# Layer 1 of a two-layer attention backbone: key copies, input splits and weight loads issued at other places

## The chip, the core and the metric

One core of a Trainium2 chip runs the whole kernel in one launch. The time is the device time of the launch in microseconds (us). TensorE (PE in the profile) does matmuls and transposes, VectorE (DVE), ScalarE (ACT) and GpSimd (POOL) do elementwise work, and SyncE (SP) issues most DMAs; ACT issues a few. Each engine executes its own list of instructions in the order in which the program was written out, and waits at an instruction whose inputs aren't there. The output is compared with a reference in fp32.

## The reference

1024 latent tokens of width 1024 (a 16 x 64 grid) and 256 context tokens go through two layers, each `x = x + gate * mixer(rms_norm(x))` with a modulation from a conditioning vector.

- Layer 0 projects to two attentions with grouped heads (one global, one in a window of 128) with rotary embedding, a SiLU gate on each, and an output projection.
- Layer 1 projects to a convolution branch (512 channels, 31 taps, layer norm, SiLU gates) and to a neighbourhood attention "d" (8 heads of 64, each query of the grid sees 8 rows x 16 columns and the context, with a bias table). Both branches are concatenated and projected:

```python
oc = conformer_conv(cv, cgl, cg, dw_w, dw_b, ln_g, ln_b)
...
y_lat = jnp.concatenate([oc, od * jax.nn.silu(dg)], axis=-1) @ w_out
```

- At the end stands a final RMS norm of the latent tokens. The change touches layer 1 only.

## The kernel before

**Arithmetic.** Everything is fp32. A matmul operand is split into a high and a low part (`split`: ACT writes the high part by a cast, L312, and POOL or DVE subtracts for the low part, L315), and a product is three matmuls (`mm3`, L334 to L336: high x high and the two mixed ones). Weights come in pieces of 128 x 256: `load_w` (L340) issues a DMA on SP into a raw buffer `wr` and splits it into `wh` and `wl`. There are `WPR` = 3 raw buffers, so a load waits until the split three pieces back is done.

**The order.** The kernel's text is traced once, and a scheduler that goes by dependences and modelled times then writes out each engine's list. `tc.issue_after(ins)` binds what is issued in its block on the engine of `ins` behind `ins`; otherwise the scheduler may put an instruction ahead of those that were written before it. `weave(main, n, fill, m)` steps two generators against each other: the attention (`main`), and projections that fill TensorE meanwhile (`fill`). `WV` holds the number of steps of each weave, `LAG` how far the fill is bound behind the attention's score matmuls.

**Layer 1's stages.** `d_proj(i)`, i = 0 to 3, projects q, k, v and the gate of the head pair i over three chunks of tokens (c = 1, 2 latent, 512 tokens each; c = 0 context, 256) and writes them to DRAM (QD, KD, VD, GD). The convolution is in the same part of the program, and its output goes to DRAM as Oc. Around `d_proj(1)` stands the layer norm of the convolution branch (its `uc`, `s`, `trs`). Then the attention runs through 16 groups (8 heads x 2 halves of the grid's columns, the order in `SEQ`), woven with `d_proj(2)`, `d_proj(3)`, then with the output projection of the convolution part (`out1_part(range(4))`, its matmuls are `po`), then of the first three head pairs (`out1_part((4, 5, 6), (1,))`), then with the ends.

**A group** (`attn_gen`, `group1`) has seven tiles of keys. Per tile: scores `st` on PE (L491 with the high parts KAt, L495 with the low parts in KBt), the bias added on DVE (`pf`, L500; not for the two context tiles), the exponential on ACT (L501, L503), `split` into `ph` (ACT) and `pl` (POOL, each fifth on DVE), and three matmuls `ov` on PE (L433 to L435). Ahead of a group its maxima are found (`mx` on PE, reduced with a bias `bm` on DVE into `mp`, then `nmt` and `QL`). In mid-group (tile 3) `gate()` loads the gate; at the last tile `last()` is called.

**Keys.** A head's keys are loaded by `load_head` into KAt at the start of the head before. `copy_k` (L580) copies the 64 high rows into KBt, one ACT cast of 64 x 1536 (L581). It is called for the next head in `last()` of each head's first half; the first head's by the `EARLY` table during `d_proj(1)`.

**The branches read back.** `out1_alloc` (L1446) allocates the tiles `oc`, `x2` and `od3`, and reads Oc back in eight DMAs of 128 x 512 on ACT's queue, each followed by its split (high on ACT, low on DVE). `od_load(hf)` (L1466) reads three pieces of 128 x 512 of the attention's output from O1d on SP's queue, each followed by its split (low on POOL). Both are called between weaves.

Of the kernel before, what the change touches and what calls it, by code (L numbers as in the profile page):

```python
# [10 lines left out]
F32 = mybir.dt.float32  # L11
# [7 lines left out]
P = 128  # L19
# [24 lines left out]
STG = {"pair": 2, "vT": 1, "spo": 2}  # L44
OCE, ODE, OHE = ('v', 'g', 'g')
YB = 1
WPR = 3
VS0 = 12
N0 = 9
NLAST = (48, 28)  # L50
# [15 lines left out]
SQP = ((2, 3, 4, 5, 6), (), (4, 6))  # L66
ENDS = ((0, 0, 512), (1, 0, 256), (1, 256, 256))
LATE = 100
EARLY = {2: lambda g, h, c: next(g[0].prep), 4: lambda g, h, c: h(0), 8: lambda g, h, c: c(),
         10: lambda g, h, c: next(g[1].prep), 14: lambda g, h, c: g[0].load_bs(), 18: lambda g, h, c: g[1].load_bs()}  # L70
NFILL = (34, 34, 34)
# [18 lines left out]
def tile_kernel(ctx: ExitStack, tc: tile.TileContext, a, out):  # L90
# [9 lines left out]
    solo = [True]  # L100
    turn = [0, 0]
    mk, mwp, hold, layer = [0], [None], [0], [0]
    sts, pvs = [], []

    def bank(tag, name):
        if tag == "pp" and solo[0]:
# [6 lines left out]
    def nm(s):  # L113
        uid[0] += 1
        return f"{s}_{uid[0]}"
# [300 lines left out]
    def attn_gen(pool, groups, vshare, look, nexts=None):  # L416
# [58 lines left out]
        for x, (g, t) in enumerate(items):  # L475
            if x + AHEAD < len(items):
                items[x + AHEAD][0].ahead(items[x + AHEAD][1])
            if t == 0:
                g.start()
                while any(p is g.prep for _, p in work):  # L480
                    prepare(len(items), 1)
                for k in g.ids:
                    next(preps[k])
                    work.append((x + LEAD[layer[0]], preps[k]))
            rate = g.rate * max(len(work), 1)
            k, q0, n, extra = g.tiles[t]
            KA, KB = g.k()
            st = bank("st", nm("st"))
            cs = slice(k * P, (k + 1) * P)
            sf = flat(st, q0, n)  # L490
            sts.append(PE.matmul(sf, KA[:, cs], cut(g.QH, q0, n), start=True, stop=False))  # L491
            if not g.bias:
                for lhs, rhs in extra():
                    PE.matmul(st[:, :n], lhs, rhs, start=False, stop=False)
            PE.matmul(sf, KB[0:68, cs], cut(g.QL[0:68], q0, n), start=False, stop=True)  # L495
            ph = pool.tile([P, 512], F32R, tag="ph", name=nm("ph"), bufs=look + 1)
            pl = pool.tile([P, 512], F32R, tag="pl", name=nm("pl"), bufs=look + 1)
            pf = pool.tile([P, 512], F32, tag="pf" if layer[0] else "ost", name=nm("pf"), bufs=PFB)
            if g.bias and extra is not None:
                VE.tensor_tensor(flat(pf, q0, n), sf, extra(), op=ALU.add)  # L500
                SC.activation(pf[:, :n], pf[:, :n], AF.Exp)  # L501
            else:
                SC.activation(pf[:, :n], st[:, :n], AF.Exp, scale=1.0 if g.bias else SCALE)  # L503
            cnt[0] += 1
            split(pf[:, :n], ph[:, :n], pl[:, :n], "s", "v" if cnt[0] % vshare == 0 else "g")
            pend.append((g, t, ph, pl))
            if t == len(g.tiles) // 2:
                g.gate()
            if t == len(g.tiles) - 1:
                g.last()  # L510
            prepare(x, rate // 2)
            yield
            if len(pend) > look:
                flush()
            prepare(x, rate - rate // 2)
            yield
# [63 lines left out]
    def copy_k(KA, KB):  # L580
        SC.copy(KB[0:64, :], KA[0:64, :].bitcast(F32))  # L581
# [370 lines left out]
    def pair(name, n=512, tag="pair"):  # L952
        return (stg[0] if tag == "spo" else lp).tile([P, 2, NR * NW], F32R, tag=tag, name=nm(name), bufs=STG[tag])[:, :, :n]
# [189 lines left out]
    with ExitStack():  # L1143
# [74 lines left out]
            w = ap.rearrange("p (r c) -> p r c", c=64)[:, :, NCOL[h_] : NCOL[h_] + NW]  # L1218
            return w.rearrange("p r (t j) -> p r t j", j=8)

        def d_proj(i):
            wsrc = (wp, WB)
            wh, wl = load_w(wsrc[0], a["od_d"], i * 512, 256, 256, wsrc[1])
            for c in (1, 2):
# [29 lines left out]
            for c in VORD:  # L1254
# [18 lines left out]
                for k0 in range(0, len(blocks), 4):  # L1273
                    bl = blocks[k0 : k0 + 4]
                    tr = bank(TRV, nm("trv"))
                    for k, (_, v) in enumerate(bl):
                        PE.transpose(tr[:, k * P : (k + 1) * P], v, ident)
                    sp = pair("spv", 640)
                    n = len(bl) * P
                    sv = sp.rearrange("p a b -> p (a b)").rearrange("p (j s d) -> p j s d", s=2, d=64)  # L1280
                    src = tr[:, :n].rearrange("p (j d) -> p j d", d=64)
                    split(src, sv[:, : 2 * len(bl), 1], sv[:, : 2 * len(bl), 0], "s", "v")
                    sv = sp.rearrange("p a b -> p (a b)").rearrange("p (j e d) -> p j e d", e=2, d=P)
                    k = 0
                    while k < len(bl):
                        e = k + 1
                        while e < len(bl) and bl[e][0] == bl[e - 1][0] + 1:
                            e += 1
                        SY.dma_start(VD[i][:, bl[k][0] : bl[k][0] + e - k], sv[:, k:e].bitcast(F32))
                        k = e  # L1290
                if c:
                    SY.dma_start(GD[i][:, :, (c - 1) * 256 : c * 256], sg.rearrange("p (h q) -> p h q", h=2))

# [37 lines left out]
        def group1(gi, hd, hf):  # L1331
# [24 lines left out]
            def gate():  # L1356
                g.gt = half("gt1")
                SY.dma_start(g.gt[ds], GD[i][ds, hf])

            def start():  # L1360
                for g2 in groups1[gi + 1 : gi + 2] if gi else ():
# [4 lines left out]
                    SY.dma_start(Vs[gi % 2][:, j : j + n, 0:128].bitcast(F32), VD[i][:, k : k + n, e])  # L1366

            def last():
                if hf == 0 and hd < 7:
                    copy_k(*heads[hd + 1])  # L1370

            def maxes(QH, mp):
                KA = Ks[hd % len(Ks)][0]
# [71 lines left out]

        def out1_alloc():  # L1446
            for c in range(2):
                ocs.append(bigp.tile([P, 2, 4, 512], F32R, tag="big", name=nm("oc")))
            for c in range(2):
                x2.append(bigp.tile([P, DK, 512], F32, tag="big", name=nm("x2")))  # L1450
                od3.append(pair("od3"))
            for c in range(2):
                for f in range(4):
                    lo = ocs[c][:, 1, f, :]
                    SC.dma_start(lo.bitcast(F32), Oc[:, f, c * 512 : (c + 1) * 512])
                    split(lo.bitcast(F32), ocs[c][:, 0, f, :], lo, "s", OCE)
                yield

        x2_of = {}

# [5 lines left out]
        def od_load(hf):  # L1466
            od[hf] = bigp.tile([P, 2, 3, 512], F32R, tag="big", name=nm("od"))
            for f in range(3):
                lo = od[hf][:, 1, f, :]
                SY.dma_start(lo.bitcast(F32), O1d[:, f, hf, :])  # L1470
                split(lo.bitcast(F32), od[hf][:, 0, f, :], lo, "s", ODE)

        def out1(fs, e, k, wh, wl, o=0, n=512):

# [87 lines left out]

        main = attn_gen(dpool, groups1, VSH, LOOK1, {11: [], 12: [13, 14], 13: [15]})
        weave(main, WV[0], d_proj(2), 31, False, True, LAG[0])
        weave(main, WV[1], d_proj(3), 31, False, True, LAG[1])
        run(out1_alloc())
        weave(main, WV[2], out1_part(range(4)), 32, False, True, LAG[2])
        assert fin[0] >= 12
        for hf in (1, 0):
            od_load(hf)  # L1570
        weave(main, WV[3], out1_part((4, 5, 6), (1,)), 8, False, True, LAG[3])
        assert fin[0] >= 14
        weave(main, WV[4], ends(EV0), NEV, False, True)
        wend = [load_w(wp, a["od_wo"], e2 * 256, 256, 256, WB, lambda dk: "gv"[dk % 2], dks=[7]) for e2 in range(4)]
# [123 lines left out]
```

## Time and profile before

| | us |
|---|---|
| median of three runs (lowest, highest) | 1540.65 (1538.62, 1540.72) |
| the profiled execution, its span | 1541.49, 1539.7 |
| PE busy (granted clock over the span) | 1444.9 (0.966) |
| DVE, POOL, ACT busy | 1109.2, 822.7, 757.4 |
| d_proj(1) with the layer norm | about 1115 to 1200 |
| d_proj(2), d_proj(3) with attention | about 1200 to 1345 |
| output projections with attention | about 1345 to 1500 |
| ends | 1500 to 1540 |

The places of the stages are read from the times of their first and last instructions. In the views, L12 is line 12 of the kernel, `out<-in` are the program's names, x8 a count, and `[4.34 <-DMA KAt<-KD]` the idle time ahead of an instruction and what ended it. PE's matmuls overlap in the pipeline: one of 512 columns is shown with 0.40 us, while the next begins 0.24 us after it. The clock that was granted to PE stands in the windows as a share of full speed.

### The profile page before, as it was taken

Reading aid. Unit: us, or ns where it says so; the run is one execution under the profiler, and the core shown is the slowest. Engines: PE = TensorE matmul, PEld = TensorE weight load, DVE = VectorE, ACT = ScalarE, POOL = GpSimd, SP = SyncE. Lnnn points to the kernel's source line nnn. Section 1 sums busy time; section 2 is a strip of 40 time slices with the busy share of each in tenths; the row PEclk is TensorE's granted clock in tenths of the full one; section 3 lists DMA queues with packets and bytes.
Section 4 is the critical chain, followed back from the end, with each engine's and each line's share of the span. In section 5 each row is a group of like instructions: output and inputs, shape, how many; then the busy total and the mean of one; then the engine's idle time right before and its main releaser. Section 6 shows DMA issues by size and latency. Waiting matters only on the chain.

```text
span 1539.7 us, 22012 instructions
## 1 busy us (share of the span) xinstructions
PE 1444.9 (94%) x6984; PEld 1172.4 (76%) x6984; DVE 1109.2 (72%) x2173; ACT 757.4 (49%) x1545; POOL 822.7 (53%) x762
## 2 busy tenths in 40 slices
PE   7889989999999999899999989999999999999994
PEld 2879868977788678678888767888878878877784
DVE  5899888588868667645478676999837665766766
ACT  3721353445453755565545665443434454544572
POOL 3361463555554775676555775664543443354664
PEclk9999989999999999999999999999999999999996
DMA  9567144423441123642111131213495677777623
GB/s 351 197 188 255 56 148 153 144 63 113 148 139 52 44 82 121 197 147 62 39 48 46 59 106 52 86 57 109 141 289 175 216 202 220 234 236 217 186 65 109
DMA packets 181163, 213.66 MB, mean 139 GB/s; under 512 B 17068, under 2 KB 134520, under 8 KB 181048
## 3 DMA queue, kind: packets, MB, share of 16 engines
q1 hardware_dynamic: 174384, 200.69, 41.7%
q10 hardware_dynamic: 6664, 11.57, 2.4%
q8 instruction: 55, 0.90, 0.3%
q14 instruction: 60, 0.49, 0.1%
HBM read 152.17 MB, written 60.03 MB: 138 GB/s over the span
## 4 chain that ended last, share of the span: by engine, by line
PE 71%; DVE 11%; DMA 6%; issue 5%; POOL 3%; ACT 2%; SPq 0%; ACTq 0%; DVEq 0%; POOLq 0%
PE p L336 7%; PE p L335 7%; PE p L334 7%; PE ov L433 4%; PE ov L435 4%; PE ov L434 4%; PE po L335 4%; PE po L334 4%; PE po L336 4%; PE st L495 3%; PE st L491 3%; PE pq L334 2%; PE pg L335 2%; PE pg L334 2%; PE pg L336 2%
## 5 line engine op out<-in xcount | busy, mean ns | idle before, releaser
L315 POOL TENSOR_TENSOR pl<-pf,ph 128x512 fp32r<-128x512 f32 (+3 forms) x321 | 392.6, 1234 | 284.2 <-ACT ph L312 218.7
L315 POOL TENSOR_TENSOR wl<-wr,wh 128x256 fp32r<-128x256 f32 (+2 forms) x256 | 193.0, 770 | 144.2 <-ACT wh L312 93.3
L503 ACT ACTIVATE pf<-st 128x512 f32<-128x512 f32 x284 | 167.1, 596 | 180.9 <-PE st L495 122.2
L312 ACT CAST ph<-pf 128x512 fp32r<-128x512 f32 (+3 forms) x364 | 206.8, 578 | 31.6 <-PE ov L434 22.5
L334 PE MATMUL p<-hh,wh 128*128 128x512 f32 x448 | 177.8, 400 | 1.6 <-ACT wh L312 1.4
L335 PE MATMUL p<-hl,wh 128*128 128x512 f32 x448 | 178.7, 401 | 0.4 <-POOL hl L315 0.4
L336 PE MATMUL p<-hh,wl 128*128 128x512 f32 x448 | 176.4, 402 | 2.1 <-POOL wl L315 2.0
L312 ACT CAST wh<-wr 128x256 fp32r<-128x256 f32 (+2 forms) x264 | 103.5, 404 | 134.1 <-DMA wr<-in_od_d_dram 29.9
L433 PE MATMUL ov<-ph,Vt 128*128 128x512 f32 (+3 forms) x364 | 143.3, 394 | 9.4 <-ACT ph L312 4.4
L491 PE MATMUL st<-QH,KAt 128*128 128x512 f32 (+3 forms) x364 | 140.6, 388 | 11.8 <-ACT pf L503 11.3
L435 PE MATMUL ov<-pl,Vt 128*128 128x512 f32 (+3 forms) x364 | 141.3, 390 | 5.4 <-POOL pl L315 5.2
L434 PE MATMUL ov<-ph,Vt 128*64 128x512 f32 (+3 forms) x364 | 139.4, 383 | 0.0
L495 PE MATMUL st<-QL,KBt 68*128 68x512 f32 (+3 forms) x364 | 137.2, 385 | 1.6 <-DVE QL L404 1.6
L1160 DVE SCALAR_TENSOR_TENSOR cps<-U,taps,cps 128x512 f32<-128x512 f32 x184 | 124.3, 749 | 0.0
L615 DVE TENSOR_REDUCE mp<-mx 128x1 f32<-128x512 f32 x128 | 86.0, 684 | 35.2 <-PE mx L614 34.3
L230 DVE SCALAR_TENSOR_TENSOR macc<-mw,csil,macc 128x512 f32<-128x512 f32 x107 | 94.5, 907 | 19.3 <-DMA mw<-in_mod_w_dram 18.4
L336 PEld LDWEIGHTS p<-hh,wl 128*128 128x128 f32 x448 | 85.3, 190 | 23.0 <-POOL wl L315 3.0
L334 PEld LDWEIGHTS p<-hh,wh 128*128 128x128 f32 x448 | 85.1, 190 | 21.8 <-ACT wh L312 1.6
L335 PEld LDWEIGHTS p<-hl,wh 128*128 128x128 f32 x448 | 85.1, 190 | 19.7 <-POOL hl L315 0.8
L491 PEld LDWEIGHTS st<-QH,KAt 128*128 128x128 f32 x364 | 69.4, 191 | 31.6 <-ACT pf L503 17.9
L433 PEld LDWEIGHTS ov<-ph,Vt 128*128 128x128 f32 x364 | 71.6, 197 | 28.7 <-ACT ph L312 8.9
L435 PEld LDWEIGHTS ov<-pl,Vt 128*128 128x128 f32 x364 | 70.7, 194 | 29.0 <-POOL pl L315 10.2
(279 smaller groups left out, 3506.7 us busy)
## 6 DMA issues: line engine op xcount, KB each, us to landing
mw<-in_mod_w_dram SPq DMA_DIRECT2D x34, 512.0 KB, 6.1
Q<-qs SPq DMA_DIRECT2D x40, 256.0 KB, 2.7
QH<-Q SPq DMA_DIRECT2D x80, 128.0 KB, 2.8
bm<-in_d_bm_dram SPq DMA_DIRECT2D x16, 540.0 KB, 5.6
wr<-in_od_d_dram SPq DMA_DIRECT2D x64, 128.0 KB, 2.7
mw<-in_mod_w_dram SPq DMA_DIRECT2D x28, 256.0 KB, 3.0
wr<-in_ev_qkv_dram SPq DMA_DIRECT2D x32, 192.0 KB, 3.8
KAt<-KD SPq DMA_DIRECT2D x16, 384.0 KB, 6.8
```

The lines of the kernel that those rows point to most:

```text
L312: SC.copy(hi, src)
L315: (GP if leng == "g" else VE).tensor_tensor(lo, src, hi.bitcast(F32), op=ALU.subtract)
L334: PE.matmul(o, lh, rh, start=first, stop=False)
L335: PE.matmul(o, lh, rl, start=False, stop=False)
L336: done[0] = PE.matmul(o, ll, rh, start=False, stop=last)
L433: PE.matmul(o, V[:, 64:192], ph, start=(t == 0), stop=False)
L434: PE.matmul(cut(g.ov[0:64], q0, n), V[:, 0:64], ph, start=False, stop=False)
L435: pvs.append(PE.matmul(o, V[:, 64:192], pl, start=False, stop=(last and g.sink is None)))
L491: sts.append(PE.matmul(sf, KA[:, cs], cut(g.QH, q0, n), start=True, stop=False))
L495: PE.matmul(sf, KB[0:68, cs], cut(g.QL[0:68], q0, n), start=False, stop=True)
L503: SC.activation(pf[:, :n], st[:, :n], AF.Exp, scale=1.0 if g.bias else SCALE)
L1160: VE.scalar_tensor_tensor(pc, uc, w, pc, op0=ALU.mult, op1=ALU.add)
```

## The change

- `WPR` goes from 3 to 5: five raw buffers for weights.
- `acs` collects the attention's exponentials, so that work can be bound behind the last one written.
- `copy_k` for heads 1 to 6 moves from `last()` of the head's first half to `gate()` of its second half, bound behind the last exponential. For head 7 it stays in `last()` of group (6, 0), bound as well; group (7, 0) is the next.
- Oc is read by two DMAs of 128 x 4 x 512 (1 MB), bound behind an exponential and issued from within `d_proj(3)`, after the part for c = 1 of the value and gate projection. The eight splits stand in a generator of their own that is merged with `d_proj(3)`, each bound behind an exponential. `out1_alloc` only allocates.
- `od_load` only loads. `od_split` is a generator, bound and merged with the output projections. The first `od_load` is called five attention steps earlier than before, the second eight steps later; `WV` is divided accordingly (27 + 8 + 9 fill steps, where 32 + 8 were).

```diff
-WPR = 3
+WPR = 5
...
+OD = 8
...
-                SC.activation(pf[:, :n], pf[:, :n], AF.Exp)
+                acs.append(SC.activation(pf[:, :n], pf[:, :n], AF.Exp))
             else:
-                SC.activation(pf[:, :n], st[:, :n], AF.Exp, scale=1.0 if g.bias else SCALE)
+                acs.append(SC.activation(pf[:, :n], st[:, :n], AF.Exp, scale=1.0 if g.bias else SCALE))
...
-        def d_proj(i):
+        def merge(first, other):
+            for _ in first:
+                yield
+                next(other, None)
+            yield from other
+
+        def d_proj(i, mid=None):
...
+                if c == 1 and mid is not None:
+                    mid()
                 if c:
                     SY.dma_start(GD[i][:, :, (c - 1) * 256 : c * 256], sg.rearrange("p (h q) -> p h q", h=2))
...
             def gate():
                 g.gt = half("gt1")
                 SY.dma_start(g.gt[ds], GD[i][ds, hf])
+                if hf == 1 and hd < 6:
+                    with tc.issue_after(acs[-1].ins):
+                        copy_k(*heads[hd + 1])
...
             def last():
-                if hf == 0 and hd < 7:
-                    copy_k(*heads[hd + 1])
+                if hf == 0 and hd == 6:
+                    with tc.issue_after(acs[-1].ins):
+                        copy_k(*heads[hd + 1])
...
         def out1_alloc():
             for c in range(2):
+                x2.append(bigp.tile([P, DK, 512], F32, tag="big", name=nm("x2")))
+                od3.append(pair("od3"))
+
+        def oc_load():
+            for c in range(2):
                 ocs.append(bigp.tile([P, 2, 4, 512], F32R, tag="big", name=nm("oc")))
             for c in range(2):
-                x2.append(bigp.tile([P, DK, 512], F32, tag="big", name=nm("x2")))
-                od3.append(pair("od3"))
+                with tc.issue_after(acs[-1].ins):
+                    SC.dma_start(ocs[c][:, 1].bitcast(F32), Oc[:, :, c * 512 : (c + 1) * 512])
+
+        def oc_split():
+            while not ocs:
+                yield
+            yield
             for c in range(2):
                 for f in range(4):
                     lo = ocs[c][:, 1, f, :]
-                    SC.dma_start(lo.bitcast(F32), Oc[:, f, c * 512 : (c + 1) * 512])
-                    split(lo.bitcast(F32), ocs[c][:, 0, f, :], lo, "s", OCE)
-                yield
+                    with tc.issue_after(acs[-1].ins):
+                        split(lo.bitcast(F32), ocs[c][:, 0, f, :], lo, "s", OCE)
+                    if f % 2:
+                        yield
...
             for f in range(3):
-                lo = od[hf][:, 1, f, :]
-                SY.dma_start(lo.bitcast(F32), O1d[:, f, hf, :])
-                split(lo.bitcast(F32), od[hf][:, 0, f, :], lo, "s", ODE)
+                SY.dma_start(od[hf][:, 1, f, :].bitcast(F32), O1d[:, f, hf, :])
+
+        def od_split(hf):
+            for f in range(3):
+                lo = od[hf][:, 1, f, :]
+                with tc.issue_after(acs[-1].ins):
+                    split(lo.bitcast(F32), od[hf][:, 0, f, :], lo, "s", ODE)
+                yield
...
-        weave(main, WV[1], d_proj(3), 31, False, True, LAG[1])
-        run(out1_alloc())
-        weave(main, WV[2], out1_part(range(4)), 32, False, True, LAG[2])
+        weave(main, WV[1], merge(d_proj(3, oc_load), oc_split()), 31, False, True, LAG[1])
+        out1_alloc()
+        low = out1_part(range(4))
+        weave(main, WV[2] - 5, low, 27, False, False, LAG[2])
         assert fin[0] >= 12
-        for hf in (1, 0):
-            od_load(hf)
-        weave(main, WV[3], out1_part((4, 5, 6), (1,)), 8, False, True, LAG[3])
+        od_load(1)
+        weave(main, OD + 5, merge(low, od_split(1)), 8, False, True, LAG[2])
+        od_load(0)
+        weave(main, WV[3] - OD, merge(out1_part((4, 5, 6), (1,)), od_split(0)), 9, False, True, LAG[3])
```

The lists of the engines show where things stand now (in the changed kernel, lines below the first few have moved by one or more: L313 is the cast L312, L316 the low part L315, L582 the key copy L581). **First place:** ACT's list in `d_proj(1)`, at the casts of the weights for v and the gate (`wh` 12078 to 12120), before:

```order
L312 CAST wh_12078<-wr_12076 128x256
L1195 ACTIVATE sql_11940<-uc_11844 128x512
L312 CAST wh_12084<-wr_12082 128x256
L312 CAST wh_12090<-wr_12088 128x256
L1195 ACTIVATE sql_11953<-uc_11844 128x512
L312 CAST spk_11966<-p_2960_11971 128x8x5x8
L581 CAST KBt_11780<-KAt_11779 64x1536
L312 CAST spk_12072<-p_2969_12027 128x256
L312 CAST wh_12096<-wr_12094 128x256
L312 CAST wh_12102<-wr_12100 128x256
L1200 COPY s_2947_11851<-bc_12015 128x512
L1206 ACTIVATE thl_12035<-uc_11844,lnbh 128x512
```

and of the change:

```order
L313 CAST wh_12078<-wr_12076 128x256
L313 CAST wh_12084<-wr_12082 128x256
L1196 ACTIVATE sql_11940<-uc_11844 128x512
L313 CAST wh_12090<-wr_12088 128x256
L313 CAST wh_12096<-wr_12094 128x256
L313 CAST wh_12102<-wr_12100 128x256
L313 CAST spk_11966<-p_2960_11971 128x8x5x8
L1196 ACTIVATE sql_11953<-uc_11844 128x512
L313 CAST spk_12072<-p_2969_12027 128x256
L313 CAST wh_12108<-wr_12106 128x256
L313 CAST wh_12114<-wr_12112 128x256
L313 CAST wh_12120<-wr_12118 128x256
```

Five weight casts stand ahead of the next that waits for PE (`spk` from `p`), where three did, and the copy of the second head's keys (11780) is gone from here; its next place is some 70 rows further on. POOL's list at the same place, with the low parts `wl` and the layer norm's `s` of the second half of the tokens (3007), before:

```order
L315 TENSOR_TENSOR wl_12079<-wr_12076,wh_12078 128x256
L1177 TENSOR_TENSOR s_3007_12163<-uc_12157 128x512
L315 TENSOR_TENSOR wl_12085<-wr_12082,wh_12084 128x256
L315 TENSOR_TENSOR wl_12091<-wr_12088,wh_12090 128x256
L248 TENSOR_TENSOR nr_11985<-rbv_11983,mhalf 128x4
L315 TENSOR_TENSOR wl_12097<-wr_12094,wh_12096 128x256
L315 TENSOR_TENSOR wl_12103<-wr_12100,wh_12102 128x256
```

and of the change:

```order
L316 TENSOR_TENSOR wl_12079<-wr_12076,wh_12078 128x256
L316 TENSOR_TENSOR wl_12085<-wr_12082,wh_12084 128x256
L316 TENSOR_TENSOR wl_12091<-wr_12088,wh_12090 128x256
L316 TENSOR_TENSOR wl_12097<-wr_12094,wh_12096 128x256
L1178 TENSOR_TENSOR s_3007_12163<-uc_12157 128x512
L316 TENSOR_TENSOR wl_12103<-wr_12100,wh_12102 128x256
L316 TENSOR_TENSOR wl_12109<-wr_12106,wh_12108 128x256
L316 TENSOR_TENSOR wl_12115<-wr_12112,wh_12114 128x256
```

Four low parts stand ahead of `s`, where one did.

**Second place:** ACT's list where the convolution branch comes back, during `d_proj(3)`, before:

```order
L1455 DMA oc_14428<-Oc 128x512
L312 CAST ph_13993<-pf_13995 128x384
L1268 ACTIVATE sgd_14051<-p_3495_14052 128x512
L1455 DMA oc_14428<-Oc 128x512 x3
L312 CAST oc_14428<-oc_14428 128x512
L1455 DMA oc_14429<-Oc 128x512
L312 CAST oc_14428<-oc_14428 128x512
L1455 DMA oc_14429<-Oc 128x512
L501 ACTIVATE pf_14029<-pf_14029 128x384
L312 CAST oc_14428<-oc_14428 128x512
L1455 DMA oc_14429<-Oc 128x512
L312 CAST ph_14027<-pf_14029 128x384
```

and of the change:

```order
L1469 DMA oc_14138<-Oc 128x4x512
L1469 DMA oc_14139<-Oc 128x4x512
L313 CAST ph_14127<-pf_14129 128x512
L504 ACTIVATE pf_14169<-st_14164 128x512
L313 CAST ph_14167<-pf_14169 128x512
L1275 ACTIVATE sgd_14230<-p_3537_14231 128x512
L502 ACTIVATE pf_14193<-pf_14193 128x128
L313 CAST oc_14138<-oc_14138 128x512 x2
L313 CAST spv_14328<-trv_14323 128x8x64
L313 CAST ph_14191<-pf_14193 128x128
L502 ACTIVATE pf_14219<-pf_14219 128x256
L313 CAST oc_14138<-oc_14138 128x512 x2
```

Eight DMAs with a cast shortly behind each became two DMAs, and the first cast stands six rows behind them; the other four casts and a key copy (11777) follow in the next six rows. On PE, `p` 3537 there is the last projection over 512 columns, so of `d_proj(3)` what PE has left behind it are the 24 matmuls of 256 columns for the context's values, and transposes.

**Third place:** ACT's list among the output projections, at the copy of a head's keys, before:

```order
L501 ACTIVATE pf_14816<-pf_14816 128x256
L312 CAST ph_14784<-pf_14786 128x384
L312 CAST ph_14814<-pf_14816 128x256
L581 CAST KBt_11777<-KAt_11776 64x1536
L503 ACTIVATE pf_14839<-st_14834 128x512
L312 CAST wh_15305<-wr_15303 128x256
L503 ACTIVATE pf_14875<-st_14870 128x512
L312 CAST ph_14837<-pf_14839 128x512
```

and the copy in the change, in mid-group:

```order
L502 ACTIVATE pf_14686<-pf_14686 128x256
L313 CAST ph_14684<-pf_14686 128x256
L502 ACTIVATE pf_14720<-pf_14720 128x384
L582 CAST KBt_11780<-KAt_11779 64x1536
L313 CAST ph_14718<-pf_14720 128x384
L1488 DMA xs_14939<-X_151 128x512
L502 ACTIVATE pf_14743<-pf_14743 128x384
L313 CAST ph_14741<-pf_14743 128x384
```

The copy stood ahead of the first exponential of the next head (`pf` from `st`, 128 x 512) and stands now behind an exponential of tile 3, with that tile's `ph` cast behind it.

More of the change, by code (lines that the diff above doesn't have):

```diff
@@ L102, in tile_kernel @@
     mk, mwp, hold, layer = [0], [None], [0], [0]
-    sts, pvs = [], []
+    sts, pvs, acs = [], [], []
     def bank(tag, name):
```

## The prediction

> **What bounds the kernel now.** I read the page's first part, then the chain of waits, then PE's waits in the stretch that the change touches, then that stretch by windows and by single instructions.
>
> ```profile
> PE 1444.9 (94%) x6984; PEld 1172.4 (76%) x6984; DVE 1109.2 (72%) x2173; ACT 757.4 (49%) x1545; POOL 822.7 (53%) x762
> ...
> PE 71%; DVE 11%; DMA 6%; issue 5%; POOL 3%; ACT 2%; SPq 0%; ACTq 0%; DVEq 0%; POOLq 0%
> ```
>
> TensorE is the bound: 94% busy, 71% of the chain. The change leaves its matmuls as they are, so it can win only where PE waits or runs at a lowered clock. PE's waits from 1100 to 1500 us (in total, times, longest):
>
> ```profile
> PE st L491 <- ACT pf L503: 2.1, 1, 2.1
> PE p L336 <- POOL wl L315: 2.0, 1, 2.0
> PE ov L433 <- ACT ph L312: 1.9, 2, 1.7
> PE ov L435 <- POOL pl L315: 1.7, 2, 1.0
> ```
>
> They are few and long, and the change has a hand in each of the four kinds. A stall also costs clock. The columns are the window, its length, the busy time of PE, PEld, DVE, ACT and POOL, the granted clock, the DMA share and GB/s:
>
> ```profile
> 1141.60:1148.60 7.00, 6.05 (x14) 4.80 (x15) 0.93 (x4) 2.25 (x3) 3.29 (x5) 0.51 1.04 385
> 1370.00:1373.80 3.80, 1.44 (x12) 1.17 (x11) 1.18 (x7) 2.13 (x6) 2.13 (x4) 1.00 0.88 225
> 1373.80:1377.40 3.60, 3.60 (x12) 2.60 (x12) 1.32 (x3) 2.04 (x5) 2.51 (x2) 0.53 0.92 297
> 1390.90:1394.40 3.50, 1.37 (x8) 1.15 (x8) 0.74 (x2) 3.35 (x6) 0.74 (x1) 0.99 1.02 236
> 1394.40:1398.00 3.60, 3.60 (x11) 3.00 (x10) 1.61 (x3) 1.89 (x5) 2.25 (x3) 0.53 1.13 302
> ```
>
> Behind each long stall comes a stretch at half clock: 7.00 x 0.49 = 3.4 us lost at the first, and twice 3.6 x 0.47 = 1.7.
>
> **Part 1: weights and the second key copy in the second d-projection (1137 to 1149 us).** What PE waited for, what stood on ACT and POOL, and how long a weight load takes:
>
> ```profile
> 1136.97 0.50 PE L334 MATMUL p<-hh,wh 128*128 128x512 f32 x1 [1.35 <-ACT wh L312]
> ...
> 1142.55 0.80 PE L336 MATMUL p<-hh,wl 128*128 128x512 f32 x1 [2.00 <-POOL wl L315]
> 1140.55 1.26 POOL L1177 TENSOR_TENSOR s<-uc 128x512 f32<-128x512 f32 x1 [2.51 <-PE trs L267]
> 1143.23 1.47 ACT L581 CAST KBt<-KAt 64x1536 fp32r<-64x1536 f32 x1 [4.34 <-DMA KAt<-KD]
> wr<-in_od_d_dram SPq DMA_DIRECT2D x64, 128.0 KB, 2.7
> ```
>
> The first weight's cast came late. The second weight's low part stood on POOL behind s, which waited for PE. The copy held ACT from 1138.9 to 1144.7 and with it the casts of the weights behind it. In the new order five weight casts instead of three stand ahead of the next thing that waits, the copy is gone from here, and on POOL four lows instead of one stand ahead of that s. Removed at most: 1.35 + 2.00 + 3.4 of clock = 6.75 us. At least 3: the last three loads still wait for a buffer, at a DMA share of 1.04. I take 5, in the upper half, since each weight serves two token tiles, and five of them give PE 5 x 6 matmuls of 0.24 us (rows in part 5), 7 us, against 2.7 us for a load.
>
> **Part 2: weights and key copies among the output projections (1369 to 1398).**
>
> ```profile
> 1369.10 0.41 ACT L312 CAST wh<-wr 128x256 fp32r<-128x256 f32 x1 [2.59 <-DMA wr<-in_od_wo_dram]
> 1371.70 0.39 PE L433 MATMUL ov<-ph,Vt 128*128 128x256 f32 x1 [1.68 <-ACT ph L312]
> 1372.88 0.39 PE L435 MATMUL ov<-pl,Vt 128*128 128x256 f32 x1 [0.68 <-POOL pl L315]
> 1391.05 1.47 ACT L581 CAST KBt<-KAt 64x1536 fp32r<-64x1536 f32 x1 [3.46 <-DMA KAt<-KD]
> 1393.06 0.39 PE L491 MATMUL st<-QH,KAt 128*128 128x256 f32 x1 [2.13 <-ACT pf L503]
> ```
>
> ACT works in order: a cast that waits for its DMA holds the exponentials and ph casts behind it. With five raw buffers a weight's load is issued two casts earlier; with the copy half a group later, its keys have landed. Removed at most: 1.68 + 0.68 + 1.7 = 4.1 and 2.13 + 1.7 = 3.8, together 7.9. At least 4, if the next late thing (a pl of POOL, a bias table) stands 1 us behind each and half the clock loss stays. I take 7, because the quoted rows name no other wait near.
>
> **Part 3: the attention output of the first three head pairs (od).** Load and split are parted, so the cast no longer stands right behind its own load:
>
> ```profile
> 1441.80 0.62 ACT L312 CAST od<-od 128x512 fp32r<-128x512 f32 x1 [2.19 <-DMA od<-O1d]
> 1441.78 0.45 PE L435 MATMUL ov<-pl,Vt 128*128 128x384 f32 x1 [1.01 <-POOL pl L315]
> ```
>
> Removed: 1.0 at most, and nothing at least, since that pl may be late behind POOL's own od work. I take 0.8. The casts' own 0.62 us lie beside the output projections' matmuls; without that cover six of them cost 3.7.
>
> **Part 4: the copies' own time.** Each is still 1.48 us of ACT, now right behind an exponential, with a ph cast queued behind it and PE's ov waiting for that.
>
> ```profile
> L581 ACT CAST KBt<-KAt x8: 1471/1478/1482, 1132.0 to 1428.2; 64x1536 fp32r<-64x1536 f32 x8
> ...
> DMA KAt<-KD: 23.9, 8
> ```
>
> 23.9 us that ACT waited ahead of eight copies gave one PE wait of 2.1 behind a copy; tiles in flight and fill matmuls hid the rest. Six copies in mid-group: 0 to 3 us, I take 0.7. Head 7's copy now stands behind the last exponential of the group directly ahead of its use, and the next st waits for it: 0 to 1.5 and 1.7 of clock, I take 1.
>
> **Part 5: the convolution branch (oc) moves from under the last large projections to behind them.** What it cost, and the work around it:
>
> ```profile
> 1300.00:1320.00 20.00, 20.00 (x103) 16.74 (x102) 10.54 (x28) 11.25 (x24) 8.71 (x11) 1.00 0.91 266
> 1320.00:1340.00 20.00, 19.25 (x103) 15.82 (x101) 17.54 (x39) 12.71 (x27) 4.85 (x5) 1.00 0.66 216
> L315 DVE TENSOR_TENSOR oc<-oc 128x512 fp32r<-128x512 f32 x8 | 6.5, 825 | 0.6 <-ACT oc L312 0.6
> L500 DVE TENSOR_TENSOR pf<-st,bs 128x384 f32<-128x384 f32 (+2 forms) x9 | 4.0, 441 | 3.9 <-PE st L495 3.8
> L1391 DVE CUSTOM_DVE_ANT_0 mx<-mx,bm 128x440 f32<-128x440 f32 (+1 forms) x7 | 3.9, 563 | 3.7 <-PE mx L1388 3.7
> L1382 DVE TENSOR_REDUCE mp<-mx 128x2 f32<-128x512 f32 x4 | 2.7, 682 | 0.0
> L312 ACT CAST oc<-oc 128x512 fp32r<-128x512 f32 x8 | 4.9, 623 | 3.9 <-DMA oc<-Oc 3.8
> L1455 ACTq DMA_DIRECT2D oc<-Oc x8: 326/335/442, 1317.4 to 1324.0; - x8
> DMA to landing us min/median/max: 3.3/4.6/5.0
> 1428.35 0.40 PE L335 MATMUL po<-oc,wh 128*128 128x512 f32 x1
> 1428.59 0.40 PE L336 MATMUL po<-oc,wl 128*128 128x512 f32 x1
> uc<-Uc SPq DMA_DIRECT2D x2, 1024.0 KB, 9.5
> X<-x SPq DMA_DIRECT2D x4, 1024.0 KB, 4.5
> ```
>
> Before, PE stayed full (20.00 and 19.25 of 20) though DVE was busy 17.54, because projection matmuls that wait for nothing filled it. In the new order PE has, between the last 512-column projection and the first output projection, some 12 us of work by 0.24 us per 512 columns (24 projection matmuls of 256 columns 2.9; ov and st of seven tiles each 5.2; mx 1.2; transposes and the rest 3). DVE has there 8 oc lows 6.5, four mx 2.3, two mp 1.4, four pf 1.8, and spv, sgd, QL and the finish of a group, by my estimate ten items at the 0.44 to 0.68 of those rows, 5: together 17. So PE would wait 5 us, less what DVE has done ahead: 2 to 5.
>
> On top of that, the first oc cast comes six ACT instructions behind the issue of two 1 MB loads, which is 5 to 7 us by the matmuls between. At 4.5 us each they are there; at 9.5 ACT stands 3 to 5 us, partly under the same stall. The 2 MB in eight pieces came between 1317.4 and 1324.0 + 5.0, at 6 us per MB, nearer the lower end. Clock adds 0 to 3.4. Lower end of the part 1 us (DVE ahead, loads in time), upper end 13; I take 5.5: 3.5 of DVE, 1 of ACT, 1 of clock.
>
> The Trainium skill says on these loads (DMA: Bandwidth & Descriptors, section Issuing engines are not separate DMA queues) that transfers started from different engines run on the same 16 DMA engines and interleave. The DMA share of 0.91 agrees that those are nearly full here; by the rule the 9.5 us end holds, this part costs about 9, and the sum below ends near -2.
>
> **The sum.** -5 - 7 - 0.8 + 0.7 + 1 + 5.5 = -5.6 us. The profiled execution took 1541.49 (span 1539.7 and 1.8 around it), 0.84 above the median of 1540.65: 1535.9 against the former, 1535 against the runs.
>
> **Rivals.**
>
> (a) Slower: the oc stage and head 7's copy take back more than the rest gives. Place: between the last projection and the first output projection. Price: 13 for the lump of DVE work and 5 for the copies, against gains of 12.8: +5, so 1546. It decides once parts 4 and 5 together pass 12.8. For it: DVE's 17.54 of 20 with the same oc work. Against it: DVE still had 2.5 us free there.
>
> (b) Nothing measurable: the stalls move. For it: 23.9 us of ACT's waiting made 2.1 of PE's, so an ACT wait is mostly hidden anyway. Against it: the half clock stands exactly behind the waits removed. Gains of 6 against costs of 6: 1540.5.
>
> (c) The full gain: 6.75 + 7.9 + 1.0 = 15.6, the oc stage hidden down to 1 and the copies free: -14.6, so 1526. For it: a load's median of 2.7 us. Against it: DVE's sum in part 5.
>
> (d) Stalls of 2 us cost no clock; the half-clock stretches have a cause that the change leaves. Then only waits go, 3.35 + 2.36 + 2.13 + 1.0 = 8.8, of which 0.82 as in my sum, 7.2; the costs without clock are 5.5: -1.7, so 1539. Against it: each stall quoted is followed by 0.51 to 0.53. The Trainium skill (TensorE: Matmul & The Clock Gate, section What's actually happening) has the clock halved after at least one idle window of about 3.4 us, by which (d) holds. The trace differs: PE was busy 1.44 of the 3.80 us ahead of the 0.53.
>
> **Chances.** Forecast 0.42, (a) 0.20, (b) 0.18, (c) 0.15, (d) 0.05. A measurement of this kernel tells about 0.2%, 3.1 us, from no change, so faster means below 1537.6 and slower above 1543.7. Faster: 0.39 of the forecast's, (c), 0.02 of (b) and 0.01 of (d), 0.57. Slower: 0.18 of (a), 0.03 of (b), 0.02 from the forecast's upper end, 0.23. The rest, 0.20, is the same. The range runs from a little below (c), 1522, to just above (a), 1547; the forecast's own is 1529 to 1540.
>
> **What would show it.** Right: a granted clock near 1.00 from 1140 to 1160, with no p waiting for wh or wl; KBt casts that no longer idle for KAt; no st or ov wait above 1 us from 1365 to 1400; and part 5 as a lower PE busy share, or a clock below 1, in the 20 us ahead of the first po, with mp, pf or ph as releasers behind oc. Wrong: PE full there, the stalls at 1137 or 1371 still in place, or one above 2 us at head 7's copy.

## The result, and the profile after

The changed kernel is half a percent slower. Its median is 1549.15 us (1541.98 to 1551.69, 11 runs) beside 1539.85 us (1534.39 to 1543.45, 11 runs) of the kernel before on the same chip, a ratio of 1.0053 with a 95% interval of 1.0033 to 1.0072: 8 us, 5 to 11. The forecast was 5.6 us less. The profiled execution took 1550.7 us, with a span of 1548.9.

The page of the profile after, busy times and chain of waits:

```profile
PE 1448.6 (94%) x6984; PEld 1175.1 (76%) x6984; DVE 1111.0 (72%) x2173; ACT 757.2 (49%) x1545; POOL 826.7 (53%) x762
...
PE 71%; DVE 12%; DMA 8%; issue 4%; POOL 2%; ACT 2%; SPq 1%; DVEq 0%; ACTq 0%; POOLq 0%
```

The engines have almost the same work (PE 1444.9 us before, DVE 1109.2); DVE and DMA have a larger part in the chain. PE's waits from 1100 to 1500 us (lines have moved: L1401 and L1393 are the maxima, L1395 and L1404 their reductions on DVE, L1518 the residual of the output projection):

```profile
PE po L335 <- DVE x L1518: 3.3, 1, 3.3
PE mx L1401 <- DVE mp L1395: 3.0, 3, 2.2
PE mx L1401 <- DVE mp L1404: 2.9, 3, 1.6
PE mx L1393 <- issue: 2.7, 1, 2.7
PE p L335 <- DVE sgd L1277: 2.5, 2, 1.3
PE st L492 <- DVE pf L501: 2.4, 3, 1.3
PE trs L268 <- DVE s L1197: 1.5, 1, 1.5
```

All four kinds that the prediction wanted gone are gone: no ACT pf, no ACT ph, no POOL wl, and pl down to 0.4 us. Others took their place, nearly all of them waits for DVE. The three places, and a fourth:

**The second d-projection (1120 to 1220).** Windows of the profile after (window, length, busy PE, PEld, DVE, ACT, POOL, clock, DMA share, GB/s):

```profile
1140.00:1160.00 20.00, 19.72 (x94) 15.91 (x92) 7.85 (x16) 4.93 (x12) 9.20 (x10) 1.00 0.67 216
1160.00:1180.00 20.00, 17.20 (x94) 13.83 (x93) 16.56 (x30) 10.06 (x21) 8.46 (x9) 1.00 0.68 234
...
1200.00:1220.00 20.00, 19.07 (x89) 15.48 (x89) 10.38 (x29) 9.74 (x27) 11.49 (x15) 0.83 0.82 252
```

The stalls at 1137 and 1142 and the half clock behind them are gone: PE is full, at clock 1.00. But from 1160 on DVE is busy 16.56 of 20 and PE waits for it (1.3 us for sgd, 1.5 for s). What is late next is DVE's part of the gate and the layer norm, where it was ACT's spv before (1.1 us at 1169). From 1200 to 1220 the clock is 0.83, about 3 us lost. That is no mark of the change: the kernel before has 0.91 there in the profile that the prediction read, and 0.83 in a second one.

**The key copies.** ACT hardly waits ahead of them any more (instructions and idle time, profile after):

```profile
L582 ACT CAST KBt<-KAt x8: 1457/1466/1474, 1132.4 to 1445.9; 64x1536 fp32r<-64x1536 f32 x8
...
DMA KAt<-KD: 3.6, 1
```

23.9 us became 3.6, as intended, and no st or ov waits over 1 us from 1365 to 1400.

**The convolution branch (1331 to 1366).** PE's waits from 1330 to 1350, two windows, and oc on DVE and in its loads, all of the profile after:

```profile
PE mx L1401 <- DVE mp L1395: 2.8, 2, 2.2
PE mx L1401 <- DVE mp L1404: 1.6, 1, 1.6
PE st L492 <- DVE pf L501: 0.9, 1, 0.9
```

```profile
1334.40:1338.40 4.00, 1.41 (x6) 0.69 (x5) 3.89 (x8) 3.46 (x9) 1.18 (x2) 1.00 0.88 286
1338.40:1348.60 10.20, 7.34 (x29) 6.39 (x30) 10.06 (x25) 6.58 (x14) 4.97 (x6) 0.50 0.45 157
```

```profile
L316 DVE TENSOR_TENSOR oc<-oc 128x512 fp32r<-128x512 f32 x8 | 5.2, 681 | 1.1 <-ACT oc L313 1.0
...
DMA oc<-Oc: 1.1, 1
...
DMA to landing us min/median/max: 7.7/7.7/7.7
```

DVE is busy 13.95 of the 14.2 us, 4.8 of them with seven of oc's eight low parts, and PE waits for the reductions and bias adds that stand between them: 2.8 + 1.6 + 0.9 = 5.3 us. The clock falls to half soon after the first and longest of these waits (2.2 us, to 1336.64); the other three lie inside the 10.2 us at half clock. PE was busy 7.34 of these, work that takes half of that at full clock, so the clock adds 3.7 us. Together these are 9.0 us. The 1 MB loads took 7.7 us, yet ACT waited only 1.1 for them. At 1361.79 stand another 3.3 us for the residual, whose load came late.

**The end of the output projections (1410 to 1466).** PE was busy 50.13 of these 56 us at clock 0.94; the two profiles of the kernel before have 53.58 and 54.73 at 1.00. By these figures 8.9 us are lost here, where 2.4 and 1.3 were. The largest wait is the 2.7 us of mx at 1430.

### The profile page after: what moved, and what is told of

It reads as the page before. It is cut to its first block, busy times and chain, and to the rows that moved or that the text cites. A ratio compares the mean times of both kernels' runs of the same rounds, so it can differ in the third digit from the quotient of the medians.

```text
span 1548.9 us, 22036 instructions
## 1 busy us (share of the span) xinstructions
PE 1448.6 (94%) x6984; PEld 1175.1 (76%) x6984; DVE 1111.0 (72%) x2173; ACT 757.2 (49%) x1545; POOL 826.7 (53%) x762
## 4 chain that ended last, share of the span: by engine, by line
PE 71%; DVE 12%; DMA 8%; issue 4%; POOL 2%; ACT 2%; SPq 1%; DVEq 0%; ACTq 0%; POOLq 0%
PE p L337 6%; PE p L336 6%; PE p L335 6%; PE ov L434 4%; PE ov L436 4%; PE ov L435 4%; PE po L335 4%; PE po L336 4%; PE po L337 4%; PE st L492 4%; PE st L496 4%; PE pq L335 2%; PE pg L335 2%; PE pq L336 2%; PE pg L336 2%
## 5 line engine op out<-in xcount | busy, mean ns | idle before, releaser
L316 POOL TENSOR_TENSOR pl<-pf,ph 128x512 fp32r<-128x512 f32 (+3 forms) x321 | 393.2, 1235 | 290.0 <-ACT ph L313 224.0
L316 POOL TENSOR_TENSOR wl<-wr,wh 128x256 fp32r<-128x256 f32 (+2 forms) x256 | 197.3, 793 | 132.4 <-ACT wh L313 90.4
L313 ACT CAST ph<-pf 128x512 fp32r<-128x512 f32 (+3 forms) x364 | 207.1, 578 | 31.9 <-PE ov L435 19.6
L313 ACT CAST wh<-wr 128x256 fp32r<-128x256 f32 (+2 forms) x264 | 101.7, 403 | 116.0 <-DMA wr<-in_ev_qkv_dram 26.3
```

The lines of the kernel that those rows point to most:

```text
L313: SC.copy(hi, src)
L316: (GP if leng == "g" else VE).tensor_tensor(lo, src, hi.bitcast(F32), op=ALU.subtract)
```

## The experiments

Theory 1: oc's splits are a lump on DVE at a place where PE has no large projection matmuls left (the 24 small ones stand in its list behind the maxima that wait, from 1343.29 on). Theory 2: the loss lies at the attention output's (od) splits and head 7's copy, where PE waits 2.7 us at 1430. Theory 3: no part alone costs much. Ratios are to runs of the kernel before on the same chip, with 95% intervals; 0.1% is 1.5 us.

| kernel | ratio to before | interval |
|---|---|---|
| the change | 1.0053 | 1.0033 to 1.0072 |
| the change, oc at its old place | 0.9990 | 0.9974 to 1.0006 |
| before, with the oc part alone | 1.0052 | 1.0034 to 1.0071 |
| the change, oc's low parts on POOL | 0.9979 | 0.9959 to 0.9999 |
| the change, oc at its old place, low parts on POOL | 0.9982 | 0.9966 to 0.9998 |
| the change, od as before | 1.0036 | 1.0019 to 1.0054 |
| the change, low parts on POOL, od as before | 0.9994 | 0.9975 to 1.0014 |
| before, five raw buffers | 0.9987 | 0.9967 to 1.0006 |
| before, key copies moved | 1.0056 | 1.0036 to 1.0076 |
| before, key copies of heads 1 to 6 moved | 1.0043 | 1.0021 to 1.0065 |
| before, key copy of head 7 bound | 0.9993 | 0.9974 to 1.0012 |
| before, five raw buffers and key copies | 0.9981 | 0.9958 to 1.0005 |
| the change, low parts on POOL, queries on ACT's queue | 1.0124 | 1.0098 to 1.0150 |

### The convolution branch back at its old place

```diff
-        weave(main, WV[1], merge(d_proj(3, oc_load), oc_split()), 31, False, True, LAG[1])
-        out1_alloc()
+        weave(main, WV[1], d_proj(3), 31, False, True, LAG[1])
+        run(out1_alloc())
```

with `out1_alloc` as in the kernel before.

> The changed kernel with the convolution branch (oc) read and split as before: eight loads with their splits after the last d-projection, nothing else undone. Theory 1 (the oc splits are a lump on DVE that stands where PE has no projection matmuls left; in the changed kernel's profile four PE waits of 2.2, 0.9, 1.6 and 0.5 us and 10.2 us at half clock, so about 10 us): 1538 to 1540, a ratio of 0.998 to 1.000 to the kernel before. Theory 2 (the loss sits at the attention output's splits and head 7's copy, 1420 to 1460 us): little changes, 1546 or more. Theory 3 (no part alone costs much, the order as a whole is worse): 1544 to 1546.

Measured: 1537.81 us, ratio 0.9990. The loss is gone, as theory 1 had it. The windows, and ACT's idle time ahead of oc:

```profile
1310.00:1330.00 20.00, 20.00 (x103) 16.71 (x102) 16.00 (x35) 12.24 (x27) 3.59 (x4) 1.00 0.68 202
1330.00:1350.00 20.00, 19.13 (x109) 15.48 (x108) 17.39 (x43) 11.01 (x26) 9.85 (x11) 1.00 0.95 281
...
DMA oc<-Oc: 5.3, 4
```

ACT waited 5.3 us for oc's loads, more than in the changed kernel, and DVE was busy 16.00 of 20 us while it had the low parts (1315.0 to 1325.1) and 17.39 behind them. PE stayed full, with the large projections running until 1327.5. The waits that the change removed on ACT cost nothing that can be measured where they stood.

### The oc part alone

The kernel before with the collected exponentials, the merged generator and the two 1 MB loads.

> The kernel before with only the oc part of the change: two loads of 1 MB, bound splits merged with the last d-projection. Theory 1: 8 to 11 us slower than before, 1548 to 1551. Theory 2: within 2 us of before. Theory 3: 3 to 5 us slower.

Measured: 1546.25 us, ratio 1.0052, 8 us, the lower end of theory 1 and about all of the change's loss. PE's waits from 1330 to 1350 and the window at half clock are nearly those of the changed kernel:

```profile
PE mx L1396 <- DVE mp L1390: 2.8, 2, 1.8
PE mx L1396 <- DVE mp L1399: 1.8, 1, 1.8
...
1342.40:1352.60 10.20, 6.99 (x27) 5.87 (x28) 10.12 (x24) 5.10 (x12) 4.30 (x5) 0.50 0.40 142
```

### Low parts on POOL

```diff
-OCE, ODE, OHE = ('v', 'g', 'g')
+OCE, ODE, OHE = ('g', 'g', 'g')
```

> The changed kernel with the eight low parts of oc subtracted on POOL instead of DVE (POOL was busy 3.6 of 20 us there, and each of its subtractions of that size took 1.29 us, so 10.3 us). If DVE's lump is what PE waits for: 6 to 10 us faster than the changed kernel, 1539 to 1543, and no PE wait for mp or pf behind oc. If ACT's eight casts or the wait for the 1 MB loads (1.1 us in the profile) are: within 2 us of the changed kernel, 1547 to 1549.

Measured: 1535.19 us, ratio 0.9979. One letter is worth 0.74%, 11 us, and the kernel is now a little faster than the one before. Casts and loads keep their places in the order of the change, and ACT's wait for the loads is nearly the same (0.8 us, 1.1 there); only the low parts are off DVE. PE's longest wait for DVE from 1325 to 1350, and the windows behind it:

```profile
PE mx L1401 <- DVE mp L1404: 1.0, 1, 1.0
...
1333.80:1337.20 3.40, 2.98 (x15) 2.98 (x15) 2.96 (x9) 3.40 (x7) 3.40 (x4) 0.50 0.77 255
1337.20:1345.00 7.80, 7.80 (x46) 6.66 (x46) 3.24 (x6) 4.56 (x12) 7.80 (x10) 1.00 0.79 225
```

So DVE's low parts are the cause, not ACT's casts and not the wait for the loads. POOL, which was busy 1.18 of 4.00 us in the changed kernel there, had the room. A stretch at half clock is left, 3.4 us instead of 10.2.

### The fourth corner

The old place and POOL together.

> The changed kernel with oc read and split at the old place (under the last large projections) and its low parts on POOL: the fourth corner beside the changed kernel (new place, DVE: 1549), the old place with DVE (1538) and the new place with POOL (1535). If the loss needs both, the new place and DVE: no better than either correction alone, 1534 to 1538. If place and engine cost independently of each other: about 11 us below either, 1525 to 1528.

Measured: 1536.42 us, ratio 0.9982. Either correction alone is enough and both together are no better, so the loss needs both: the low parts on DVE, and the place without large projections.

### The attention output's splits

The change with `od_load` and the weaves behind it as before.

> The changed kernel with the attention output's load and split, and the division of the steps among the output projections, as before. Theory 2: the waits at 1423 and 1430 and the half clock at 1430 and 1454 us go, 5 to 7 us faster than the changed kernel, 1542 to 1544. Theory 1: within 2 us of the changed kernel.

Measured: 1544.59 us, ratio 1.0036. It is 0.17% below the change, 2.6 us, less than theory 2 asked, and the intervals overlap. In the profile the half clock from 1410 to 1466 is gone, and the wait of 2.7 us at 1430 is down to 0.7, as theory 2 had it. With the low parts on POOL the same step went the other way:

> The changed kernel with oc's low parts on POOL and with the attention output's load, split and steps as before. If the two corrections add up (13.6 us and 4 us below the changed kernel by the runs before this): 1531 to 1533. If the od part's loss was only a consequence of the lump ahead of it: 1534 to 1537, no better than the low parts alone.

Measured: 1536.66 us, ratio 0.9994, 0.15% above the low parts on POOL alone, the second expectation. So an effect of the od part of either sign can't be told here. Theory 2 falls as the account of the 8 us: either correction of oc takes the loss away with the od part left in.

### Five raw buffers, and the key copies

```diff
-WPR = 3
+WPR = 5
```

> The kernel before with five raw weight buffers instead of three, nothing else. If the weights' waits of the profile before (1137 to 1149 and 1369 to 1377 us) are real costs that five buffers remove: 6 to 10 us faster, 1529 to 1533. If what is late next takes their place (in the changed kernel's profile sgd, s and a clock drop of 6.8 us between 1165 and 1209): 0 to 3 us faster, 1536 to 1539.

Measured: 1534.73 us, ratio 0.9987 with an interval that holds 1: 2 us, the second expectation. PE's waits from 1100 to 1500:

```profile
PE p L334 <- DVE sgd L1270: 2.4, 2, 1.3
PE po L334 <- ACT od L312: 2.3, 1, 2.3
PE st L491 <- DVE pf L500: 1.8, 4, 1.1
PE mx L1380 <- DMA KAt<-KD: 1.5, 1, 1.5
PE trs L267 <- DVE s L1196: 1.5, 1, 1.5
PE mx L1380 <- DMA QH<-QD: 1.4, 2, 1.0
```

No wait for wh or wl is left; od, pf, KAt, s, QH and a second sgd are late in their stead.

> The kernel before with the key copies moved as in the change (heads 1 to 6 into the gate of the second half, head 7 bound), nothing else. If the copy's wait at 1391 is a real cost: 3 to 5 us faster, 1534 to 1536. If tiles in flight hide it in most executions: within 2 us of before. If head 7's bound copy costs by itself: 2 to 4 us slower.

Measured: 1546.23 us, ratio 1.0056. The third expectation, a loss, came out, but of 8 to 9 us where it said 2 to 4. Whether head 7's copy makes it, as it also said, was asked with two more kernels:

> The kernel before with the copies for heads 1 to 6 moved into mid-group and head 7's left unbound in the last tile's call, as before. Key copies alone (both moves) were 8 us slower than before. If head 7's binding makes that loss (its profile has mx waiting 3.9 us for KAt at 1432 and 6.8 us of half clock at 1453): the loss goes, 1537 to 1541. If the copies in mid-group make it, by the order that follows from them (waits for QH, mp and pf at 1262, 1376 and 1381): 1544 to 1548.

> The kernel before with only head 7's copy bound behind the exponential of the last tile, heads 1 to 6 as before. If head 7's binding makes the loss: 1544 to 1548. If the copies in mid-group make it: 1537 to 1541.

Measured: heads 1 to 6 alone 1544.11 us, ratio 1.0043; head 7 alone 1534.28 us, ratio 0.9993. The copies in mid-group make the loss, not head 7's. ACT's idle time ahead of the copies and PE's waits, with heads 1 to 6 alone:

```profile
DMA KAt<-KD: 6.3, 2
...
PE mx L1383 <- DMA KAt<-KD: 3.6, 1, 3.6
PE mx L1391 <- DVE mp L1394: 2.6, 3, 1.6
PE mx L1383 <- DMA QH<-QD: 2.4, 2, 1.6
```

ACT's waiting fell from 23.9 us to 6.3, and the kernel became 7 us slower: in this profile the maxima wait for their key and query loads and for their reductions. That they come too early, by the changed order of the matmuls ahead of them, is argued, not shown.

> The kernel before with five raw buffers and the moved key copies, oc and od as before. By the terms of the prediction's sum (5 and 7 off, 1.7 on): 10 us faster, 1529. If gains are eaten by what is late next: 0 to 3 us faster, 1536 to 1539, about the sum of the two runs alone.

Measured: 1534.47 us, ratio 0.9981, interval 0.9958 to 1.0005: some 3 us, not 10, and not the sum of the two alone (2 less and 9 more). With five buffers the copies' loss does not appear. Why the two act together so stays open.

### Queries on ACT's queue

Where the low parts were on POOL, PE's longest remaining waits were mx for QH and for the key and query loads of head 7. SP waits 45 to 67 us for raw weight buffers in these profiles, in order, so the query loads were put on ACT's queue.

```diff
-                SY.dma_start(QH[0:64, :].bitcast(F32), QD[i][ds, 0, hf])
+                SC.dma_start(QH[0:64, :].bitcast(F32), QD[i][ds, 0, hf])
```

and so for the other two.

> The changed kernel with oc's low parts on POOL, and layer 1's query loads (QH, QL) issued on ACT's queue instead of SP's. If the queries are late because SP, in order, waits for raw weight buffers ahead of them (45 to 67 us of SP's waits in the profiles): mx no longer waits for QH (1.1, 2.0 and 1.8 us in the run with the low parts on POOL, and 3.4 us of half clock), 3 to 6 us below that run, 1529 to 1532. If it is the DMA engines' share or the buffer that makes them late: within 2 us of it, 1533 to 1537.

Measured: 1557.98 us, ratio 1.0124, a miss on both sides. PE waits more for QH, not less:

```profile
PE mx L1393 <- DMA QH<-QD: 5.1, 4, 1.7
```

The largest loss stands elsewhere, at the start of the attention: from 1200 to 1220 PE was busy 11.36 of 20 us at clock 0.63, where the run with the low parts on POOL has 19.52 at 0.90. Its cause was not followed up. SP's queue as the cause of the late queries is not supported, and not excluded either, since on ACT's queue the loads stand behind whatever ACT waits for.

### The kernel before, profiled a second time

> The kernel before, unchanged, for a second profile. If the six long stalls of the first profile (1137, 1142, 1371, 1372, 1393, 1441 us) are fixed costs of its order: all return within 0.5 us of their lengths. If some depend on when DMAs happen to land: one to three of them are gone or halved, others stand elsewhere, and the sum of 15.6 us that the prediction removed was one execution's.

Measured: 1536.1 us, span 1534.3. PE's waits from 1100 to 1500, and windows in the stages of the prediction's parts 1 and 2:

```profile
PE p L334 <- ACT spv L312: 2.6, 1, 2.6
PE p L336 <- POOL wl L315: 2.0, 1, 2.0
...
PE ov L435 <- POOL pl L315: 1.4, 2, 0.7
PE st L491 <- ACT pf L503: 1.3, 1, 1.3
PE ov L433 <- ACT ph L312: 1.3, 1, 1.3
...
1142.00:1149.00 7.00, 4.97 (x26) 4.11 (x26) 1.02 (x5) 1.86 (x2) 3.61 (x4) 1.00 1.04 336
...
1160.00:1180.00 20.00, 17.44 (x91) 14.78 (x90) 13.78 (x28) 10.19 (x24) 5.80 (x8) 0.91 0.71 236
...
1200.00:1220.00 20.00, 19.01 (x93) 15.73 (x92) 13.62 (x38) 10.69 (x27) 11.05 (x14) 0.83 0.87 275
...
1373.20:1377.00 3.80, 3.80 (x22) 3.11 (x22) 2.23 (x5) 2.47 (x6) 2.53 (x2) 1.00 0.86 280
```

The second expectation. The wait for wh (1.35) is gone, wl (2.0) is there, ph is 1.3 where 1.68 was, pf 1.3 where 2.13 was, pl 0.7 each. And the half clock behind them (3.4 + 1.7 + 1.7 us) is not there: the same three places run at 1.00. What the prediction counted as 15.6 us is 2.0 + 1.3 + 0.7 + 1.3 + 0.7 = 6.0 in this execution.

In the second d-projection, though, the loss has moved and not gone. PE waits 2.6 us for spv at 1170, where it waited 1.1, and half clock follows (0.91 from 1160 to 1180); from 1200 to 1220 the clock is 0.83, where it was 0.91. From 1120 to 1220 PE is busy 94.4 of 100 us at a mean clock of 0.95 in both profiles. Among the output projections the loss did go: from 1366 to 1410 PE is busy 39.51 of 44 us at 0.92 in the first profile and 40.69 at 1.00 in the second.

## Why the prediction was wrong

The place and the mechanism of the loss were foreseen, in part 5 and as rival (a). What failed are the sizes on both sides: the gains of parts 1 and 2 were put at 12 us and came to 3, and part 5 was put at 5.5 and cost 8 to 11. Step by step:

- **What bounds the kernel.** Right: PE's work is unchanged, and the differences found are waits and clock of PE.
- **The signs.** Nearly all that were named for being right were there: the clock at 1.00 from 1140 to 1160, no wait for a weight above 0.3 us, one KBt cast idle for KAt instead of eight, no st or ov wait above 1 us from 1365 to 1400, and part 5's lower share of PE with mp and pf as releasers. They watch the waits that go and not those that come in their place, so they could not tell a gain from a loss.
- **Part 1 (5 us off).** The stalls at 1137 and 1142 went, as did the clock loss. It failed as a saving: five buffers alone gave 2 us (0.9987, interval 0.9967 to 1.0006). The step that failed is that a removed wait and its half clock were counted as time won (its 3.4 us of clock were nearer 3.0 even so, since PE was busy 6.05 of the 7.00 us). DVE's sgd and s became late next (1.3 + 1.5 us; the other sgd wait of 1.1 stood there before), and the 3.4 us of clock and the 1.35 us wait were one execution's; in the other, as much was lost at other points of the stage. From 1120 to 1220 PE was busy 94.4 us at 0.95 before, 95.5 at 0.95 with five buffers alone and 95.1 at 0.97 in the change.
- **Part 2 (7 us off).** The sentence "the quoted rows name no other wait near" failed: with five buffers alone PE waits 1.0 us for QH at 1373.84 and 1.1 for DVE's pf at 1384.47. And 3.4 of its 7.9 us were clock that the second profile doesn't have. Five buffers and key copies together are worth 3 us, where the sum had 12 off and 1.7 on.
- **Part 3 (0.8 off).** Can't be told: two comparisons of it have opposite signs.
- **Part 4 (0.7 and 1 on).** Head 7's binding costs nothing that can be measured. The copies in mid-group, sized 0 to 3, cost 7 us on three buffers (1.0021 to 1.0065); on five that loss doesn't show. The quoted row (23.9 us of waiting on ACT, 2.1 on PE) said that most of ACT's waiting is hidden, and taking it away won nothing that can be measured. Rival (b) had that right.
- **Part 5 (5.5 on).** Right mechanism, about half the size: 11 us by the low parts on POOL, 10 by the old place, 8 alone on the kernel before. Its terms were 3.5 of DVE, 1 of ACT, 1 of clock; the profile has 5.3, nothing that is seen on PE, and 3.7. So the clock term was the one most mis-sized: four waits of 0.5 to 2.2 us within 9 us came with half clock for 10.2 us, where the term took 1 out of 0 to 3.4. The wait at 1361.79 for a residual's load, 3.3 us, wasn't in the sum. The loads took 7.7 us, between the two ends, and ACT waited 1.1. The rule of the Trainium skill on shared DMA engines (DMA: Bandwidth & Descriptors, Issuing engines are not separate DMA queues) didn't decide it: the part did cost about the 9 us that were worked out for late loads, but through DVE and the clock.
- **The sum.** 12.8 off and 7.2 on were to be 5.6 off; the runs have about 3 off and 11 on, 8 on. The upper end of part 5 (13) was kept for the range, but set against gains of 12.8, so the range ended at 1547.
- **Rival (a)** named the place, the engine and 1546. That 1546 came near the measured 1549 is luck in the sizes: it set 13 and 5 of cost against 12.8 of gain, and the runs have 8 to 11, nothing measurable for head 7's copy, and 3. Its point of decision, 12.8 us of loss, was wrong with the gains: 3 would do. **Rival (d)**, that short stalls cost no clock in themselves, has the second profile for it (2.0 us of waiting and clock 1.00 behind it) and two places against it: the wait for spv in the same profile, and the oc stage (0.50 in the change and in the oc part alone). Neither always nor never.

## What to carry to other kernels

Ahead of moving elementwise work, ask what the bound engine has to do at the new place, not how idle the helper engines are on average: under free projection matmuls 5 us of DVE work and 5 us of DMA waiting cost nothing that could be measured, and behind these matmuls the same DVE work cost about 10. Before moving it, try the engine that is idle there; here that was one letter. And a wait on an engine off the path, however long its row, is worth only what the bound engine waits for it; take the stalls to be removed from two profiles, since some of them, and above all the half clock behind them, belong to one execution. And sum what the bound engine loses over the whole stage: a wait that is gone from its row may stand a few microseconds on.

## What the runs showed of the hardware

The half clock of TensorE did not follow a stall of a given length. Behind a 2.0 us wait it stood at 0.51 for 7 us in one execution of the kernel before and at 1.00 in another, with the same instructions; the first of these also had a wait of 1.35 us, which ended 3.6 us ahead. In the second, a wait of 2.6 us at 1170 was followed by half clock. In a cluster of waits it stood at 0.50 for 10.2 us though PE was busy 7.34 of them; with the oc part alone it was 10.2 and 6.99.

Executions of one kernel on one chip mostly spread over some 10 us (15 for the one with the low parts on POOL, 1527.58 to 1543.05 in 12 runs), as much as the effects asked for; no single pair of profiles could have told any of these comparisons.
